# A hybrid RWKV-7 and sparse-attention layer on one core: gates of two token groups projected ahead of the choice of keys, and the choice dealt out differently

## The chip, the core and the metric

The kernel runs on one core of a Trainium2 chip. The metric is device time in microseconds (us) of one execution; the kernel before took 2103.36 us, the median of three runs (2098.55 to 2105.53). The core's engines are PE (matmul, with its weight loads shown as PEld), DVE, ACT, POOL and SP; each works through its own instructions strictly in the order in which the built program holds them. SP issues nearly all DMAs.

## What is computed

One layer on 2048 tokens of width 1024, all in 32-bit floats. `p = rmsnorm(x) @ w_in`, and the columns of `p` go two ways:

```python
p_shift, g_rwkv, q_down, kv_down, k_idx_raw, w_idx, g_attn = jnp.split(p, IN_SPLITS, axis=-1)
y_rwkv = rwkv7_branch(p_shift, g_rwkv, ...)     # r, k, v, decay, a from p_shift; a scan over time; * silu(gate)
y_attn = dsa_branch(q_down, kv_down, k_idx_raw, w_idx, g_attn, ...)
y = jnp.concatenate([y_rwkv, y_attn], axis=-1) @ w_out        # then x + y, and a last rmsnorm
```

The scan runs over 2048 steps with 8 heads of 64. The attention branch first scores all earlier keys of each query with a small index (4 heads of 64), keeps the best 256 of them (`lax.top_k`), and attends to those alone, with 8 heads over a shared latent. Both branches end in a product with `silu` of a gate, 512 columns each (`g_rwkv`, `g_attn`).

## The kernel before

The program has three parts that the scheduler of the framework orders on each engine by priority (the order of the source, unless `later` lowers it) and by its own idea of durations. The result is one fixed order per engine.

**Projections and choice** (`phase_as`). Tokens are worked in four groups of 512. `x_group` (L541) normalises and transposes a group into two tiles `xh`, `xl` (high and low part of the split floats, two buffers each). `proj` (L573) multiplies 128 columns of `w_in` with a group: 24 matmuls of 128x512, eight each on lines 577 to 579, into one of three PSUM tiles `pm`. `load_w` (L524) brings such a weight through one raw buffer and splits it into `wh` (ACT, L535) and `wl` (DVE, L536), three buffers each. `index_proj` and `index_group` (L645, L655) make the index keys, index weights and queries of a group with three projections. A job then uses a finished `pm`: `gate` (L809) takes its SiLU on ACT (L812) and stores it; `shifted`, `keys`, `lora` and `latent` mix neighbouring tokens (L586 on ACT, L588 on DVE), normalise and store.

`visit` (L823) walks over 22 such weights in rounds, each weight for two groups; at its end `x_again` (L567) loads the next two groups. `choose` (L434) makes for each of 14 blocks of 128 queries the scores (L246 and L247 on PE, L249 on ACT, L252 and L254 on DVE; two buffers `xs`) and, at lower priority, `quick` (L271): twelve steps of a search for the threshold, each one pass over the scores with a count, on ACT and POOL for even blocks (L317, L321, L323, L314), on DVE for odd blocks (L320 and the same small lines), and then a tail on DVE (L329 to L346) that fixes ties and stores the block's mask (L347). The blocks come in the order 14, 15, 12, 13, 10, 11, 8, 9, 6, 7, 2, 3, 4, 5. `mix` (L854) takes one share of the choice (one block's scores) after each round of a visit.

```python
for i, g in enumerate(order):            # 2, 3, 0, 1
    t, qr = index_proj(g, ws)
    index_group(g, t, qr)
    if i < 2:
        x_group(order[i + 2])
```

**Scan** (`phase_r`). Sixteen batches of 128 tokens. `prep` (L931, twice a batch) loads `ld` (L937), works on DVE and PE (L950 to L984) and scales on POOL (L987); `systems` sends small triangular systems through DRAM (`du`, then `A`, L1017); `inverse` (L1021) solves them on POOL in 31 steps (L1031, L1033), writes `dx` and reads `TT`; `chain` (L1041) multiplies with `TT` on PE (L1068) and carries the state. Its tiles take the memory of the projections, so it begins when the last projection is finished.

**Attention and output** (`phase_t`, `phase_w`). Units of one head pair and one query block, scores and values by key blocks of 128 (L1261, L1262 scores; L1263 mask and maximum on DVE; L1295 transposes; L1304 value products), then the product with `w_out` (L1381 to L1384). Their priority is lower than the scan's, so they fill its gaps; what is left is done behind it.

Of the kernel before, what the change touches and what calls it, by code (L numbers as in the profile page):

```python
# [475 lines left out]
def phase_as(env):  # L476
# [6 lines left out]
    def tl(shape, dt, tag, bufs=1):  # L483
        return pa.tile(shape, dt, name=nm(tag), tag=tag, bufs=bufs)

    def pst(shape, tag, bufs=1):
        return ps.tile(shape, F32, name=nm(tag), tag=tag, bufs=bufs)

    def t2(dt=F32):
        return tl([128, 512], dt, "t2", 6)  # L490

    def tls(shape, dt, tag, bufs=1):
        return e.ps_.tile(shape, dt, name=nm(tag), tag=tag, bufs=bufs)
# [30 lines left out]
    def load_w(cols, pad=False, raw=None):  # L524

        if raw is None:
            raw = tl([128, KD, 128], F32, "wraw", 1)
        src = e.w_in[0].rearrange("(k p) c -> p k c", p=128)
        if pad:
            G.memset(raw, 0.0)  # L530
        for t0, s0, w in cols:
            dma(raw[:, :, t0:t0 + w], src[:, :, s0:s0 + w])
        wh = tl([128, KD, 128], F32R, "wh", 3)
        wl = tl([128, KD, 128], F32R, "wl", 3)
        S.activation(wh, raw, AF.Copy)  # L535
        V.tensor_tensor(wl, raw, f32(wh), op=OP.subtract)  # L536
        return wh, wl
# [3 lines left out]
    def x_group(g):  # L541
        xh = tl([128, KD, 512], F32R, "xh", 2)
        xl = tl([128, KD, 512], F32R, "xl", 2)
        XH[g], XL[g] = xh, xl
        for tb in range(4 * g, 4 * g + 4):
            xt = tls([128, T], F32, "xs", 2)[:, :D] if tb % 4 >= 2 else tl([128, D], F32, "xt", 2)
            dma(xt, e.x[0, tb * 128:(tb + 1) * 128, :])
            st = tl([128, 4], F32, "xst", 4)
            tcol = slice((tb % 4) * 128, (tb % 4) * 128 + 128)
            S.activation(xl[:, :, tcol], xt.rearrange("p (k c) -> p k c", k=KD), AF.Square, accum_out=st[:, 0:1])  # L550
            V.tensor_scalar(st[:, 1:2], st[:, 0:1], 1.0 / D, 1e-6, op0=OP.mult, op1=OP.add)
            rpow(st[:, 2:3], st[:, 1:2])
            V.scalar_tensor_tensor(xt, xt, st[:, 2:3], gb, op0=OP.mult, op1=OP.mult)
            for hf in range(2):
                pt = pst([128, 4, 128], "tr", 2)
                for k in range(4):
                    kk = hf * 4 + k
                    PE.transpose(pt[:, k], xt[:, kk * 128:(kk + 1) * 128], ident)
                sl = (slice(None), slice(hf * 4, hf * 4 + 4), slice((tb % 4) * 128, (tb % 4) * 128 + 128))
                S.activation(xh[sl], pt, AF.Copy)  # L560
                V.tensor_tensor(xl[sl], pt, f32(xh)[sl], op=OP.subtract)

        if g >= 2:
            dma(e.d_x[g - 2][0], f32(xh))
            dma(e.d_x[g - 2][1], f32(xl))
# [7 lines left out]
    def proj(w, g):  # L573
        wh, wl = w
        pm = pst([128, 512], "pm", 3)
        for k in range(KD):
            PE.matmul(pm, wh[:, k], XH[g][:, k], start=k == 0, stop=False)  # L577
            PE.matmul(pm, wh[:, k], XL[g][:, k], start=False, stop=False)  # L578
            PE.matmul(pm, wl[:, k], XH[g][:, k], start=False, stop=k == KD - 1)  # L579
        return pm  # L580
# [64 lines left out]
    def index_proj(g, ws):  # L645
        t = t2()
        S.activation(t[0:68], proj(ws[0], g)[0:68], AF.Copy)
        qr, sqs = [], []
        for j in range(2):
            pm = proj(ws[1 + j], g)  # L650
            qr.append(t2())
            S.activation(qr[j], pm, AF.Copy)
        return t, qr
# [80 lines left out]
    def latent_weights():  # L734

        raw = tl([128, KD, 128], F32, "wraw", 1).rearrange("p a b -> p (a b)").rearrange("p (a b) -> p a b", a=2)
        dma(raw[:, 0].rearrange("p (h d) -> p h d", h=8), e.w_uk[0].rearrange("h r d -> r h d"))
        dma(raw[:, 1].rearrange("p (h d) -> p h d", h=8), e.w_uv[0].rearrange("h r d -> r h d"))
        for i, n in enumerate(("wh", "wl")):
            ukv[i] = tl([128, KD, 128], F32R, n, 3).rearrange("p a b -> p (a b)").rearrange("p (a b) -> p a b", a=2)  # L740
        split(raw, ukv[0], ukv[1])
# [74 lines left out]
    jobs = dict(kv=([(0, C_KV, 128)], latent), lora=([(0, C_WD, 64), (64, C_WD, 64)], lora))  # L816
# [6 lines left out]
    def visit(gs, rounds, nxt=()):  # L823

        late = []
        for i, names in enumerate(rounds):
            some = [(load_w(jobs[n][0]), jobs[n][1]) for n in names.split()]
            if "kv" in names.split():
                latent_weights()
            for gi, g in enumerate(gs):  # L830
                for w, job in some:
                    pm = proj(w, g)
                    for _ in range(2):
                        if late:
                            late.pop(0)()
                    f = job(pm, g)
                    if f:
                        late += f if isinstance(f, list) else [f]
                if i == len(rounds) - 1:
                    while late:  # L840
                        late.pop(0)()
                    if nxt:
                        x_again(nxt[gi])
            yield

    def index_weights():
        raws = tls([128, 2, KD, 128], F32, "xm", 1)
        ws = [load_w([(0, C_KI, 64), (64, C_WI, 4)], pad=True)]
        if not hasattr(e, "kig"):
            e.__dict__.update(e.vectors())  # L850
            env.update(e.__dict__)
        return ws + [load_w([(0, C_QD + j * 128, 128)], raw=raws[:, j]) for j in range(2)]

    def mix(*gens):  # L854

        while next(gens[0], gens) is not gens:
            for x in gens[1:]:
                next(x, None)

    order = (2, 3, 0, 1)  # L860
    x_group(2)
    ws = index_weights()
    query_weights()
    x_group(3)
    for i, g in enumerate(order):
        t, qr = index_proj(g, ws)
        index_group(g, t, qr)
        if i < 2:
            x_group(order[i + 2])
    lora_weights()  # L870
    stored = dma(e.d_ki, f32(KI))
    with tc.issue_after(stored.ins):
# [3 lines left out]
    shares = choose((7, 6, 5, 4, 3, 1, 2))  # L876
    for _ in range(2):
        next(shares)
    mix(visit((0, 1), ["r0 gr0 k0", "lora v0 ga0", "kv r1", "gr1 k1", "v1 ga1", "r2 gr2", "k2 v2", "ga2 r3", "gr3 k3",
                       "v3 ga3"], (2, 3)), shares)  # L880
    mix(visit((2, 3), ["r0 gr0 k0", "lora v0 ga0", "kv r1", "gr1 k1", "v1 ga1", "r2 gr2", "k2 v2", "ga2 r3 gr3",
                       "k3 v3 ga3"]), shares)
    for _ in shares:
        pass

# [534 lines left out]
```

## Time and profile before

| | us |
|---|---|
| median of three runs | 2103.36 |
| the profiled execution | 2104.7 |
| its span in the profile | 2102.9 |
| PE busy / weight loads busy | 1803.3 (86%) / 1421.8 (68%) |
| DVE busy | 1296.7 (62%) |
| ACT busy | 1019.8 (48%) |
| POOL busy | 795.3 (38%) |

The span is the time from the first to the last instruction of the program; 1.8 us of the execution lie around it. Busy times are unions of an engine's instructions; matmuls overlap in their pipeline, so PE's is not a measure of its work. A row of a view of time windows gives for each engine its busy us and (after x) its number of instructions, then the granted share of PE's clock (1.00 is 2.4 GHz, 0.50 is 1.2 GHz; a stretch between shows both), the DMA engines' busy share and GB/s.

### The profile page before, as it was taken

Reading aid. Unit: us, or ns where it says so; the run is one execution under the profiler, and the core shown is the slowest. Engines: PE = TensorE matmul, PEld = TensorE weight load, DVE = VectorE, ACT = ScalarE, POOL = GpSimd, SP = SyncE. Lnnn points to the kernel's source line nnn. Section 1 sums busy time; section 2 is a strip of 40 time slices with the busy share of each in tenths; the row PEclk is TensorE's granted clock in tenths of the full one; section 3 lists DMA queues with packets and bytes.
Section 4 is the critical chain, followed back from the end, with each engine's and each line's share of the span. In section 5 each row is a group of like instructions: output and inputs, shape, how many; then the busy total and the mean of one; then the engine's idle time right before and its main releaser. Section 6 shows DMA issues by size and latency. Waiting matters only on the chain.

```text
span 2102.9 us, 36153 instructions
## 1 busy us (share of the span) xinstructions
PE 1803.3 (86%) x12906; PEld 1421.8 (68%) x12906; DVE 1296.7 (62%) x3050; ACT 1019.8 (48%) x1966; POOL 795.3 (38%) x1925
## 2 busy tenths in 40 slices
PE   5788998879796988986788988886988889899998
PEld 4666877658575867765566766665766667587776
DVE  5532538979779698986656557564756654644432
ACT  4422494453444744441355555454655567643431
POOL 1110124353544354562445645654546650100000
PEclk9778999989798999998799998798988899999999
DMA  7526334332262434234844355343454324744223
GB/s 248 199 94 200 108 101 135 101 115 85 75 239 63 135 107 136 91 95 125 204 102 105 95 136 147 105 119 98 115 143 131 93 78 108 233 128 128 66 93 112
DMA packets 309038, 262.50 MB, mean 125 GB/s; under 512 B 82544, under 2 KB 258288, under 8 KB 307696
## 3 DMA queue, kind: packets, MB, share of 16 engines
q1 hardware_dynamic: 304464, 248.03, 40.1%
q0 software_dynamic: 4384, 12.06, 1.8%
q8 instruction: 104, 1.70, 0.4%
q14 instruction: 86, 0.70, 0.1%
HBM read 166.37 MB, written 97.85 MB: 126 GB/s over the span
## 4 chain that ended last, share of the span: by engine, by line
PE 23%; POOL 14%; DMA 12%; issue 5%; DVE 4%; SPq 1%; ACT 1%; POOLq 0%; DVEq 0%; ACTq 0%
DMA A<-du 6%; POOL Xr L1033 6%; POOL Xtmp L1031 5%; PE om L1304 3%; PE po L1381 3%; PE po L1382 3%; PE po L1384 3%; PE tr L1295 3%; DMA dx<-Xr 2%; PE s L1261 2%; PE s L1262 1%; DMA TT<-dx 1%; DMA ld<-d_rw 1%; POOL yo L1129 1%; POOL gst L1112 1%
## 5 line engine op out<-in xcount | busy, mean ns | idle before, releaser
L577 PE MATMUL pm<-xh,wh 128*128 128x512 f32 x800 | 330.4, 414 | 20.3 <-DVE t L588 11.8
L578 PE MATMUL pm<-xl,wh 128*128 128x512 f32 x800 | 327.0, 409 | 0.0
L579 PE MATMUL pm<-xh,wl 128*128 128x512 f32 x800 | 326.1, 408 | 0.0
L1263 DVE CUSTOM_DVE_ANT_0 sc<-s,mk 128x512 f32<-128x512 f32 (+3 forms) x320 | 187.9, 607 | 102.8 <-PE s L1262 76.0
L1297 ACT ACTIVATE pt<-tr 128x512 f32<-128x512 f32 (+1 forms) x288 | 157.9, 569 | 160.8 <-PE tr L1295 115.9
L1031 POOL TENSOR_TENSOR Xtmp<-Xr,A 128x60 f32<-128x60 f32 (+24 forms) x496 | 146.9, 296 | 225.8 <-DMA A<-du 181.8
L577 PEld LDWEIGHTS pm<-xh,wh 128*128 128x128 f32 x800 | 158.1, 198 | 61.7 <-DVE t L588 13.7
L1270 ACT ACTIVATE sc<-sc,mx 128x128 f32<-128x128 f32 (+15 forms) x128 | 153.0, 1198 | 63.0 <-DVE mx L1269 62.7
L1295 PE MATMUL tr<-ident,sc 128*128 128x128 f32 x1088 | 180.1, 292 | 3.0 <-ACT pt L1297 2.6
L579 PEld LDWEIGHTS pm<-xh,wl 128*128 128x128 f32 x800 | 157.3, 197 | 36.4
L578 PEld LDWEIGHTS pm<-xl,wh 128*128 128x128 f32 x800 | 158.0, 197 | 35.4
L1304 PE MATMUL om<-pt,vt 128*64 128x128 f32 x2176 | 174.0, 295 | 6.2 <-DVE ga L1287 6.2
L1261 PE MATMUL s<-kt,q 128*128 128x512 f32 (+2 forms) x320 | 144.2, 454 | 35.8 <-DVE mx L1263 32.2
L1033 POOL TENSOR_TENSOR Xr<-Xr,Xtmp 128x60 f32<-128x60 f32 (+24 forms) x496 | 151.3, 305 | 37.4
L1304 PEld LDWEIGHTS om<-pt,vt 128*64 128x64 f32 x2176 | 134.2, 146 | 37.6 <-issue 19.6
L1295 PEld LDWEIGHTS tr<-ident,sc 128*128 128x128 f32 x1088 | 133.5, 149 | 33.9 <-issue 11.4
L317 ACT ACTIVATE mk<-x,st 128x1920 bf16<-128x1920 f16 (+5 forms) x72 | 98.0, 1361 | 103.6 <-POOL st L314 103.6
L249 ACT ACTIVATE rl<-lg,wi 128x512 f32<-128x512 f32 (+3 forms) x152 | 94.0, 631 | 99.6 <-PE lg L247 53.1
L1262 PE MATMUL s<-kt,q 128*128 128x512 f32 (+2 forms) x320 | 123.3, 389 | 8.1 <-DMA q<-d_q 8.0
L320 DVE TENSOR_SCALAR_CACHE_REDUCE mk<-x,st 128x2048 bf16<-128x2048 f16 (+5 forms) x72 | 120.6, 1675 | 1.4
L254 DVE SCALAR_TENSOR_TENSOR xs<-rl,wi,xs 128x512 f32<-128x512 f32 (+3 forms) x108 | 73.5, 681 | 60.9 <-ACT rl L249 60.1
L1387 POOL TENSOR_TENSOR st<-st 128x1 f32<-128x1 f32 x16 | 3.1, 195 | 277.1 <-ACT po L1386 277.1
(329 smaller groups left out, 3937.7 us busy)
## 6 DMA issues: line engine op xcount, KB each, us to landing
wraw<-in_w_in_dram SPq DMA_DIRECT2D x42, 512.0 KB
d_rw<-t SPq DMA_DIRECT2D x80, 256.0 KB
ld<-d_rw SPq DMA_DIRECT2D x32, 640.0 KB
q<-d_q SPq DMA_DIRECT2D x128, 128.0 KB
d_q<-t SPq DMA_DIRECT2D x32, 256.0 KB
d_kt<-t SPq DMA_DIRECT2D x32, 256.0 KB
kt<-d_kt SPq DMA_DIRECT2D x32, 256.0 KB
A<-du SPq DMA_DIRECT2D x16, 512.0 KB
```

The costliest lines, as they stand in the source:

```text
L577: PE.matmul(pm, wh[:, k], XH[g][:, k], start=k == 0, stop=False)
L578: PE.matmul(pm, wh[:, k], XL[g][:, k], start=False, stop=False)
L579: PE.matmul(pm, wl[:, k], XH[g][:, k], start=False, stop=k == KD - 1)
L1031: G.tensor_tensor(tmp[:, :m, :w], Xr[:, :m, s:s + 1].to_broadcast([128, m, w]), A[:, s:s + 1, s + 1:].to_broadcast([128, m, w]), op=OP.mult)
L1033: m_ = G.tensor_tensor(Xr[:, :m, s + 1:], Xr[:, :m, s + 1:], tmp[:, :m, :w], op=OP.add)
L1261: PE.matmul(pS[:, :wp], qh[:, h, qs], k[:, h, :wp], start=True, stop=False)
L1262: PE.matmul(pS[:, :wp], ql[:, h, qs], k[:, h, :wp], start=False, stop=True)
L1263: V.tensor_tensor_reduce(out=rows[h][:, c0:c0 + w], in0=pS[:, :w], in1=mk[:, c0:c0 + w], scale=1.0, scalar=LOW, op0=OP.add, op1=OP.max, ac ...
L1270: marks[p, b] = S.activation(rows[h][:, :n], rows[h][:, :n], AF.Exp, bias=mx[:, h, 4:5], accum_out=sums[:, h:h + 1]).ins
L1295: PE.transpose(pt[:, i, h], rows[h][:, (kb + i) * 128:(kb + i) * 128 + 128], ident)
L1297: S.activation(w[:, :m], pt[:, :m], AF.Copy)
L1304: PE.matmul(po[HALF[h]], v[:, (kb + i) % 4, HALF[h]], w[:, i, h], start=kb + i == 0, stop=kb + i == b)
```

## The change

The eight gate weights (`gr0` to `gr3`, `ga0` to `ga3`) of groups 2 and 3 are taken out of the second visit and projected in a function of their own, `gates`, between the index groups of 2 and 3 and the loading of groups 0 and 1. The index weights are loaded a second time behind them, since the gates use their buffers. The second visit has 14 weights in 7 rounds instead of 22 in 9. `mix` skips a share after two rounds of the first visit (numbers 3 and 6) and after three of the second (2, 4 and 6).

```diff
-    def mix(*gens):
-
-        while next(gens[0], gens) is not gens:
-            for x in gens[1:]:
-                next(x, None)
+    def mix(main, other, skip):
+
+        for i, _ in enumerate(main):
+            if i not in skip:
+                next(other, None)
+
+    def gates(gs, rounds):
+
+        for names in rounds:
+            some = [(load_w(jobs[n][0]), jobs[n][1]) for n in names.split()]
+            for g in gs:
+                for w, job in some:
+                    job(proj(w, g), g)
...
-    for i, g in enumerate(order):
+    for g in order[:2]:
         t, qr = index_proj(g, ws)
         index_group(g, t, qr)
-        if i < 2:
-            x_group(order[i + 2])
+    gates(order[:2], ["gr0 ga0 gr1", "ga1 gr2", "ga2 gr3 ga3"])
+    ws = index_weights()
+    for g in order[2:]:
+        x_group(g)
+    for g in order[2:]:
+        t, qr = index_proj(g, ws)
+        index_group(g, t, qr)
...
     mix(visit((0, 1), ["r0 gr0 k0", "lora v0 ga0", "kv r1", "gr1 k1", "v1 ga1", "r2 gr2", "k2 v2", "ga2 r3", "gr3 k3",
-                       "v3 ga3"], (2, 3)), shares)
-    mix(visit((2, 3), ["r0 gr0 k0", "lora v0 ga0", "kv r1", "gr1 k1", "v1 ga1", "r2 gr2", "k2 v2", "ga2 r3 gr3",
-                       "k3 v3 ga3"]), shares)
+                       "v3 ga3"], (2, 3)), shares, (3, 6))
+    mix(visit((2, 3), ["r0 k0", "lora v0 r1", "kv r2", "r3 v1", "v2 v3", "k1 k2", "k3"]), shares, (2, 4, 6))
```

The order on the engines changes with it; lines behind L860 have numbers 12 higher in the changed file. On ACT, behind the queries of group 3 (L623, from `pm`): before, the copies of the transposed tokens of group 1 (L560) and the next index projection (L647) follow.

```order
L623 ACTIVATE t_142_848<-pm_841 128x512
L560 ACTIVATE xh_867<-tr_918 128x4x128
L623 ACTIVATE t_145_861<-pm_854 128x512
L560 ACTIVATE xh_867<-tr_925 128x4x128
L560 ACTIVATE xh_867<-tr_939 128x4x128
L647 ACTIVATE t_165_953<-pm_954 68x512
```

In the changed program, at the same place, the gates' SiLUs (L812) and weight splits (L535) stand, and the tokens of group 0 behind them:

```order
L623 ACTIVATE t_127_775<-pm_768 128x512
L812 ACT_TABLE_LOAD
L812 ACTIVATE t_139_824<-pm_799 128x512
L812 ACTIVATE t_141_852<-pm_827 128x512
L812 ACTIVATE t_143_880<-pm_855 128x512
L535 ACTIVATE wh_969<-wraw_967 128x1024
...
L812 ACTIVATE t_182_1246<-pm_1221 128x512
L521 ACTIVATE w2s_134<-wraw_1878 128x1024
L535 ACTIVATE wh_1292<-xm_1277 128x1024
L812 ACTIVATE t_184_1274<-pm_1249 128x512
L560 ACTIVATE xh_1296<-tr_1305 128x4x128
```

All sixteen gates of the two groups moved there; on PE their projections stand in one run behind the last query projection of group 3.

On SP's queue, where the scan begins (`ld`, `vt`), before: the stores of the last projections (`d_rw`, `d_v`, `d_ga`), the scan's first loads, and attention's first loads (`kt`).

```order
L813 DMA d_ga<-t_1340_7737 128x512
L798 DMA d_rw<-t_1336_7702 128x512
L806 DMA d_v<-t_1338_7708 128x512
L937 DMA ld_7779<-d_rw 128x10x128
L943 DMA vt_7780<-d_v 128x2x128
...
L1124 DMA gr_8762<-d_gr 128x2x128
L1221 DMA kt_13715<-d_kt_68 64x2x512
```

In the changed program the masks of blocks 7, 2 and 3 (L347, 1024, 384 and 512 keys) are stored between the last projection's stores and the scan's first load; those of blocks 4 and 5 and the first write of `dx` come ahead of attention's first load:

```order
L347 DMA d_mask_78<-mk_5656 128x1024
L798 DMA d_rw<-t_1348_7756 128x512
L347 DMA d_mask_73<-xt_5953 128x384
L347 DMA d_mask_74<-xt_6360 128x512
L949 DMA ld_7798<-d_rw 128x10x128
...
L347 DMA d_mask_75<-mk_6984 128x640
...
L1046 DMA dx_7887<-Xr_7888 4x256x32
L347 DMA d_mask_76<-mk_7548 128x768
L1050 DMA TT_7958<-dx_7887 32x8x32 x4
...
L1233 DMA kt_13734<-d_kt_68 64x2x512
```

The end of the choice moved behind the end of the projections, and the scan's first load behind the mask of block 3.

## Rows read from the trace of the kernel before

**Rows 1.** Time windows by stage: window, its length, then busy us by engine.

```profile
core 0: us, PE busy (x) PEld busy (x) DVE busy (x) ACT busy (x) POOL busy (x), PEclk, DMA share, GB/s
0.00:201.00 201.00, 150.59 (x664) 120.49 (x665) 91.45 (x210) 72.69 (x132) 23.63 (x36) 0.85 0.53 178
201.00:601.00 400.00, 353.44 (x1507) 280.27 (x1506) 282.92 (x407) 208.73 (x288) 152.42 (x266) 0.92 0.36 116
601.00:979.00 378.00, 331.81 (x1457) 265.13 (x1455) 321.86 (x651) 173.70 (x289) 187.43 (x381) 0.94 0.34 111
979.00:1068.00 89.00, 53.99 (x314) 40.15 (x313) 50.33 (x175) 30.26 (x81) 27.06 (x89) 0.73 0.80 193
1068.00:1740.00 672.00, 571.04 (x6579) 445.07 (x6580) 393.71 (x1209) 371.77 (x848) 377.54 (x1093) 0.88 0.43 112
1740.00:2100.00 360.00, 342.44 (x2392) 270.70 (x2390) 156.41 (x399) 162.69 (x330) 27.26 (x62) 0.98 0.41 126
```

**Rows 2.** Time windows of line 577 alone (PE, then weight loads).

```profile
201.00:601.00 400.00, 146.57 (x353) 70.12 (x353) 0.92 0.36 116
601.00:979.00 378.00, 144.86 (x352) 69.19 (x351) 0.94 0.34 111
```

**Rows 3.** Timeline of PE inside a projection: start, us, instruction.

```profile
937.61 0.39 PE L577 MATMUL pm<-xh,wh 128*128 128x512 f32 x1
...
939.01 0.39 PE L577 MATMUL pm<-xh,wh 128*128 128x512 f32 x1
```

**Rows 4.** Timelines of DVE, SP, POOL and PE at the end of the phase.

```profile
959.93 0.96 DVE L331 MAX8 st<-xm 128x8 f32<-128x768 f32 x1
...
966.09 0.56 DVE L346 TENSOR_TENSOR mk<-mk,eq 128x768 bf16<-128x768 bf16 x1
...
979.76 0.74 DVE L588 SCALAR_TENSOR_TENSOR t<-pm,om_r,m 128x512 f32<-128x512 f32 x1
...
981.01 0.58 SPq L937 DMA_DIRECT2D ld<-d_rw  x1
...
1024.96 0.24 POOL L1031 TENSOR_TENSOR Xtmp<-Xr,A 128x31 f32<-128x31 f32 x1 [18.57 <-DMA A<-du]
...
1068.11 0.41 PE L1068 MATMUL ch<-R,TT 32*32 32x64 f32 x2 [8.40 <-DMA TT<-dx]
```

**Rows 5.** Waits of 1050 to 1740 (total, times, longest), and line 1031 on its own.

```profile
POOL Xtmp L1031 <- DMA A<-du: 163.2, 13, 17.2
...
L1031 POOL TENSOR_TENSOR Xtmp<-Xr,A x496: 209/292/745, 1025.0 to 1730.1; 128x60 f32<-128x60 f32 x16, 128x28 f32<-128x28 f32 x12, 128x66 f32<-128x66 f32 x11, 128x48 f32<-128x48 f32 x10
```

**Rows 6.** Time windows in the holes of the early stage.

```profile
95.00:110.00 15.00, 8.38 (x39) 7.00 (x39) 11.35 (x28) 7.87 (x17) 5.15 (x6) 0.61 0.00 0
116.00:126.00 10.00, 4.66 (x25) 4.13 (x23) 2.24 (x4) 1.18 (x3) 0.68 (x1) 0.66 0.68 211
...
180.30:192.30 12.00, 6.49 (x32) 5.58 (x31) 6.76 (x19) 4.09 (x8) 2.02 (x2) 0.64 0.35 90
```

**Rows 7.** Groups by line and form on DVE, 201 to 979: busy, mean ns.

```profile
L536 DVE TENSOR_TENSOR wl<-wraw,wh 128x1024 fp32r<-128x1024 f32 x41 | 50.1, 1222 | 24.0 <-ACT wh L535 24.0
```

**Rows 8.** Groups by line on ACT, 201 to 979.

```profile
L535 ACT ACTIVATE wh<-wraw 128x1024 fp32r<-128x1024 f32 x41 | 43.3, 1055 | 44.2 <-DMA wraw<-in_w_in_dram 26.8 <-PE pm L578 15.2 <-PE pm L579 2.0
...
L812 ACT ACTIVATE t<-pm 128x512 f32<-128x512 f32 x32 | 18.9, 591 | 26.2 <-PE pm L579 16.3 <-DMA d_kt<-t 9.7 <-PE tr L776 0.2
```

**Rows 9.** Groups by line and form on DVE, 890 to 979: a search step of block 5.

```profile
L320 DVE TENSOR_SCALAR_CACHE_REDUCE mk<-x,st 128x768 bf16<-128x768 f16 x12 | 12.1, 1008 | 0.3
...
L314 DVE TENSOR_SCALAR st<-st 128x1 f32<-128x1 f32 x15 | 4.1, 271 | 0.9 <-POOL st L312 0.5
...
L321 DVE TENSOR_SCALAR st<-st 128x1 f32<-128x1 f32 x16 | 3.4, 210 | 0.3
```

**Rows 10.** Timeline of PE in the last stage: value products and transposes of attention.

```profile
1898.40 1.97 PE L1304 MATMUL om<-pt,vt 128*64 128x128 f32 x32
...
1903.17 1.09 PE L1295 MATMUL tr<-ident,sc 128*128 128x128 f32 x8
```

## Prediction

> **What bounds the kernel now.** I read the profile from coarse to fine: the stages of the span, then who holds up whom at the two seams that the change touches.
>
> The page gives one busy share per engine over the whole span, a mean over stages with different limits; the busy time by stage [rows 1] separates them. From 0 to 201 us, while the four groups are prepared, DVE works 91 us of 201 and PE has holes. From 201 to 601 (visit of groups 0 and 1) and from 601 to 979 (visit of groups 2 and 3) the projections and the choice of keys share the engines: DVE is busy 283 of 400 us, then 322 of 378. From 979 the scan starts alone; from 1068 to 1740 its chain runs with attention filled in; after 1740 PE does attention and the output product at 342 of 360 us.
>
> That the visits are these stretches is seen by counting: a projection has 8 matmuls of line 577, and the two visits hold 353 and 352 of them [rows 2], which is 44 projections each; the early stage has the 12 of the index. A projection at full clock costs 24 matmuls that start 0.233 us apart (937.61 to 939.01 for six) [rows 3], so 5.6 us. The 44 of the second visit are thus 246 us of PE in 378; the matmuls' busy time of 332 us is larger because they overlap. DVE's 322 us do not overlap. **In the second visit DVE is nearer to its limit than PE.**
>
> By the raw busy row PE (332) would lead DVE (322), and taking gates out would give PE's share back: that is the second case below, 2110 us. The Trainium skill (Perfetto Trace Analysis, "Identifying the Most-Contended Engine") says that matmul busy time is no measure of PE's headroom, and to take the weight loads' busy share there and plain occupancy for VectorE. Here that gives 265 of 378 (70%) against 85%, so by that rule VectorE leads and the forecast, 2150 us, is the one to take. The same page ("Optimization Strategy") advises interleaving regimes with different limits, which speaks against a stretch of gates by themselves.
>
> At the end of the phase the last DVE operation of the choice ends at 966.7, the last shift of a projection on DVE starts at 979.76, SP issues the scan's first load at 981.01, the first triangular inverse starts on POOL at 1024.96 and the first product with it on PE at 1068.11 [rows 4]. The scan's stage is then paced by a loop through POOL and DMA: POOL waits 163 us there for A [rows 5].
>
> **The change, part by part.** The profiled execution took 2104.7 us (span 2102.9); the median of the three runs is 2103.4, so sums on the profile are 1.3 us high.
>
> 1. *Sixteen gates go in front of the choice.* The choice of the first blocks needs the index keys of all four groups, so all of it, and both visits, start later by what the gates take. In the built order they stand in one block after the index group of group 3, not in the holes of the early stage (95 to 110, 116 to 126, 180.3 to 192.3, where PE is busy 20 of 37 us [rows 6]). Sixteen at 5.6 us are 90 us. The two token loads of groups 0 and 1 stood in the holes of groups 2 and 3; now they stand behind the gates, whose last three projections cover their squares. What the hole of group 3 loses in width (it runs on to 126 [rows 6]) comes back behind the gates. I take plus 90, ends 78 and 102: the visits start at 291 instead of 201.
>
> 2. *Weights.* Eight gate weights are split earlier (8 x 1.22 us of DVE [rows 7], 8 x 1.06 of ACT [rows 8]) and three index weights are loaded once more, 512 KB each, through SP's queue during the gates. A split frees the weight buffer after at most 2.3 us and the gates use a weight for 11.2 us, so PE covers them: 0. Without that cover the three would cost 3 x 2.3 = 7 us. The gates' sixteen SiLUs (0.59 us [rows 8]) and stores go with them; they run beside PE: 0.
>
> 3. *First visit.* Its rounds are unchanged, and on DVE the built order has the choice at the same places between the same projections: block 13 ends before the last key projection in both, although two shares are skipped, since only two score buffers exist. So 400 us again, until 691.
>
> 4. *Second visit.* Twenty-eight projections are left. DVE's work behind the start of the visits is 283 + 322 = 605 us [rows 1]; 10 us of weight splits leave it. In the built order SP stores the mask of block 3 ahead of the scan's first load, and blocks 4 and 5 end on DVE after that; ten of twelve search steps of block 5 (1.01 us each, and three small operations of 0.21 to 0.27 [rows 9]: 18 us) and two block tails (that of block 5 ran from its pass for the largest values at 959.93 to 966.65 [rows 4], 6.7 us, and one pass more stands ahead of it: 15 us for two) are left behind the load, 33 us in all. So 605 - 10 - 33 - 283 = 279 us of DVE must pass between 691 and the load. At the second visit's 85% that takes 328 us, without any idle 279. PE has 16 x 5.6 = 90 us less to do there, so some of DVE's waits for PE go, but those inside the choice (score to ReLU to sum, POOL to ACT) stay. I take 90%: 310 us, and the load at about 1003: **plus 22** against 981. Ends with those of part 1: minus 15 and plus 50.
>
> 5. *Head of the scan.* Before, 87 us lie between the first load and the first product, at a DMA share of 0.80 [rows 1] because attention's loads run in front on the same queue. Now those loads come behind the first inverse, but 33 us of DVE work and the last POOL steps of block 4 come in front of it. Both unknown; the idle in that stretch is 39 of 89 us on DVE, so most of the 33 fits: 0, ends minus 12 and plus 15.
>
> 6. *Attention starts later.* It now begins behind the first product instead of well ahead of it. On PE the built order has 742 of the 1088 value products of attention ahead of the scan's last matmul, 816 before: 74 more are left, which is 37 pairs of a query and a key block. One pair is 8 products of 64 columns in the trace's halves (1.97 us for 32 records: 0.25 us), two transposes (1.09 us for 8: 0.27) and 512 columns of scores (0.23) [rows 10]: 0.75 us, 28 in all, at the end where PE has 18 of 360 us idle. I take **plus 24**, ends 10 and 28. From the second pair of scan batches to the last, the built order has 694 products before and 688 now, so the loop between keeps its pace.
>
> Sum: 2104.7 + 22 + 0 + 24 = 2151, about **2150 us** as a median. Its own range, part by part, is 2122 to 2182.
>
> **The other ways it could go.**
>
> *PE was the limit of the second visit.* Then DVE runs without idle once the gates are gone: load at 291 + 400 + 283 = 974, minus 7; the head gains 10 without attention's loads; attention's remainder still costs 24: about 2110 us. For it: PE waits little in the second visit, 332 of 378 busy. Against: 246 us of projections in 378, and DVE at 85%.
>
> *Faster: the scan's stage is paced by PE.* Besides the case just told (load 974, head minus 10), the 37 pairs taken out of the stage would shorten it by the 28 us that they cost later, so the two cancel: 2104.7 - 7 - 10 = about 2088. It decides from an inverse cadence under 44 us; now the 16 x 31 steps run from 1025.0 to 1730.1 [rows 5], some 45 us a batch. For it: PE busy 571 of 672 [rows 1]. Against: the 163 us for which POOL waits for A [rows 5].
>
> *Slower still: the head is stretched.* POOL's and DVE's in-order queues put block 4's and block 5's serial steps between the scan's preparations, each waiting for the other; plus 15 in the head, the load at the far end, plus 50: about 2190. For it: from 1068 to 1740, where two kinds of work share every queue as they would here, no engine but PE is busy for 60% (DVE 394 of 672 us) [rows 1]. Against: PE and ACT are nearly free in the head.
>
> That the change does not do what it says is half a rival: the gates fill no hole, and the choice is hardly spread. Both are in the forecast.
>
> **How the numbers follow.** Forecast (2122 to 2182) 0.58; PE the limit 0.15; faster 0.10; slower still 0.17. Of the second case, which lies at plus 0.3% with some 10 us either way, I count 0.07 as no change (within 0.3%, or 6 us, about what a measurement can tell) and 0.08 as slower. Slower: 0.58 + 0.17 + 0.08 = 0.83; same 0.07; faster 0.10. For eight in ten the range reaches down to the second case and up to the near side of the fourth: 2108 to 2186.
>
> **What would show it.** In the new profile: a stretch of 16 gates with PE full and DVE nearly empty, some 90 us; the first scores of the choice near 300; the second visit shorter than 378 us but by less than 90; the scan's first load near 1003, behind the store of block 3's mask; the first attention score after the first inverse; cadence of the inverses unchanged; more attention behind the scan's end. The prediction is wrong if the scan's first load comes before 980, or if the visits start before 275.

## The result and the profile after

The changed kernel takes 2169.07 us (median; 2166.88 to 2171.27), the kernel before, run beside it, 2100.95 (2097.73 to 2105.53): a ratio of 1.0323, with a 95% interval of 1.0307 to 1.0339, so it is slower by 68 us. The forecast was 2150, its range 2108 to 2186. The profiled execution has a span of 2167.2 us and took 2169.0.

The busy time of the profile after by stage, with the columns of [rows 1]. The first row and the third make up the early stage of before with the gates in it, and the row of 114 to 204 is the gates alone:

```profile
0.00:294.00 294.00, 242.88 (x1048) 193.47 (x1049) 105.80 (x221) 94.13 (x160) 23.68 (x37) 0.89 0.48 155
...
114.00:204.00 90.00, 90.00 (x391) 73.00 (x390) 16.82 (x18) 23.20 (x34) 4.01 (x5) 1.00 0.25 79
204.00:294.00 90.00, 75.28 (x319) 58.68 (x318) 38.75 (x75) 30.74 (x56) 7.67 (x10) 0.79 0.41 129
...
294.00:696.00 402.00, 354.13 (x1508) 280.59 (x1507) 285.13 (x410) 208.40 (x288) 154.88 (x267) 0.92 0.36 117
696.00:948.00 252.00, 228.22 (x1010) 183.22 (x1009) 218.68 (x387) 125.55 (x203) 124.62 (x254) 0.95 0.37 123
948.00:1014.00 66.00, 17.18 (x64) 12.50 (x62) 62.09 (x179) 22.16 (x48) 44.36 (x96) 0.53 0.09 34
1014.00:1097.00 83.00, 29.16 (x148) 20.74 (x148) 58.76 (x162) 13.48 (x33) 42.93 (x121) 0.52 0.36 96
1097.00:1741.00 644.00, 542.77 (x6177) 422.17 (x6175) 393.72 (x1198) 359.19 (x835) 356.17 (x1027) 0.88 0.49 123
1741.00:2167.00 426.00, 399.76 (x2959) 314.02 (x2959) 183.69 (x501) 200.86 (x401) 48.86 (x128) 0.97 0.39 119
```

Read it from the top. For 90 us PE does gates without a pause while DVE is busy 17: that stretch is new. The first visit is as long as before (402 against 400). The projections of the second visit end at 948, 252 us after its start instead of 378. But then comes a stretch that the kernel before did not have: from 948 to 1014 DVE is busy 62 of 66 us, PE 17, at a granted clock of 0.53. The projections' matmuls are done and the choice is not.

The seam, by the timelines of DVE (ends of blocks 7, 2, 3, 4 and 5), SP, POOL and PE (the second PE row is attention's first score):

```profile
983.80 0.68 DVE L346 TENSOR_TENSOR mk<-mk,eq 128x1024 bf16<-128x1024 bf16 x1
995.43 0.35 DVE L346 TENSOR_TENSOR xt<-xt,eq 128x384 bf16<-128x384 bf16 x1
1012.65 0.41 DVE L346 TENSOR_TENSOR xt<-xt,eq 128x512 bf16<-128x512 bf16 x1
1049.99 0.47 DVE L346 TENSOR_TENSOR mk<-mk,eq 128x640 bf16<-128x640 bf16 x1
1083.87 1.45 DVE L346 TENSOR_TENSOR mk<-mk,eq 128x768 bf16<-128x768 bf16 x1
...
1013.10 0.32 SPq L347 DMA_DIRECT2D d_mask<-xt  x1
1013.58 0.59 SPq L949 DMA_DIRECT2D ld<-d_rw  x1
1085.34 7.73 SPq L347 DMA_DIRECT2D d_mask<-mk  x1
1094.99 1.78 SPq L1050 DMA_DIRECT2D TT<-dx  x4
...
1097.47 1.25 SPq L1233 DMA_DIRECT2D kt<-d_kt  x2
...
1056.20 0.24 POOL L1043 TENSOR_TENSOR Xtmp<-Xr,A 128x31 f32<-128x31 f32 x1 [11.86 <-DMA A<-du]
...
1096.79 0.42 PE L1080 MATMUL ch<-R,TT 32*32 32x64 f32 x2 [8.92 <-DMA TT<-dx]
1106.86 0.77 PE L1273 MATMUL s<-kt,q 128*128 128x256 f32 x2 [0.81 <-DMA ga<-d_ga]
```

Against [rows 4]: the choice's last operation starts at 1084 instead of 966, the scan's first load is issued at 1013.6 instead of 981.0, right behind the store of block 3's mask, and attention's first load at 1097. On SP that one stands behind the store of block 5's mask, whose issue took 7.73 us, and behind the scan's own loads of `TT`, so here both the choice's end and the first inverse lie just ahead of it; e7 separates them. The span divides into four: the load 32.6 us later; from the load to the first product 83.2 us instead of 87.1; from there to the scan's last product 727.4 instead of 724.5; behind it 343.0 instead of 310.3. Sum: 32.6 - 3.9 + 2.9 + 32.7 = 64.3, the difference of the spans.

What the last term is made of shows in the PE groups behind the scan's last product, first after (from 1824), then before (from 1792): transposes and value products of attention.

```profile
L1307 PE MATMUL tr<-ident,sc 128*128 128x128 f32 x338 | 54.3, 283 | 4.5 <-ACT pt L1309 4.0 <-ACT sc L1282 0.5
L1316 PE MATMUL om<-pt,vt 128*64 128x128 f32 x692 | 49.1, 283 | 1.7 <-DVE ga L1299 1.7
```

```profile
L1295 PE MATMUL tr<-ident,sc 128*128 128x128 f32 x266 | 40.2, 277 | 1.0 <-ACT pt L1297 0.9
L1304 PE MATMUL om<-pt,vt 128*64 128x128 f32 x544 | 37.9, 284 | 1.5 <-DVE ga L1287 1.5
```

692 value products instead of 544 are left, 148 more, which is 4 for each of the 37 pairs that the prediction counted.

### The profile page after: what moved, and what is told of

Same layout as the page of the kernel before. It is cut to its first block, busy times and chain, and to the rows that moved or that the text cites. A ratio compares the mean times of both kernels' runs of the same rounds, so it can differ in the third digit from the quotient of the medians.

```text
span 2167.2 us, 36188 instructions
## 1 busy us (share of the span) xinstructions
PE 1814.1 (84%) x12906; PEld 1426.7 (66%) x12906; DVE 1307.9 (60%) x3053; ACT 1023.8 (47%) x1964; POOL 795.5 (37%) x1926
## 4 chain that ended last, share of the span: by engine, by line
PE 34%; POOL 21%; DMA 14%; DVE 14%; issue 9%; ACT 5%; SPq 2%; POOLq 0%; ACTq 0%; DVEq 0%
POOL Xr L1045 6%; POOL Xtmp L1043 6%; DMA A<-du 6%; PE pm L577 4%; PE pm L578 4%; PE pm L579 4%; PE po L1393 3%; DVE mk L320 3%; PE po L1394 3%; PE po L1396 3%; PE om L1316 2%; PE tr L1307 2%; PE s L1273 2%; DMA dx<-Xr 2%; ACT mk L317 1%
## 5 line engine op out<-in xcount | busy, mean ns | idle before, releaser
L1316 PE MATMUL om<-pt,vt 128*64 128x128 f32 x2176 | 167.1, 291 | 2.3 <-DVE ga L1299 2.3
L1316 PEld LDWEIGHTS om<-pt,vt 128*64 128x64 f32 x2176 | 129.3, 144 | 32.9 <-issue 20.1
L536 DVE TENSOR_TENSOR wl<-wraw,wh 128x1024 fp32r<-128x1024 f32 x46 | 56.2, 1222 | 86.8 <-ACT wh L535 86.8
```

The costliest lines, as they stand in the source:

```text
L1316: PE.matmul(po[HALF[h]], v[:, (kb + i) % 4, HALF[h]], w[:, i, h], start=kb + i == 0, stop=kb + i == b)
```

## The experiments

Three theories stood against each other. **The choice** (its work on DVE, with POOL and ACT) ends when it ends, whatever PE has to do, and the scan and attention wait for it. **PE's projections** set the phase. **The order** that the change brings with it (dealing, mask stores on SP, keys last) is the cost. In the table "first pass" is the start of the choice's first L292 on DVE, "choice ends" its last L346; all times are of one profiled execution of each, in us; the ratio is of the medians, to the kernel before on the same chip. "Left" counts value products of attention behind the scan's last product.

| kernel | ratio, 95% interval | first pass | choice ends | scan's first load | attention's first score | scan's last product | behind it | left |
|---|---|---|---|---|---|---|---|---|
| before | 1 | 254.9 | 966 | 981 | 997 | 1793 | 310 | 544 |
| after | 1.0323 [1.0307, 1.0339] | 347.8 | 1084 | 1014 | 1107 | 1824 | 343 | 692 |
| e1, no dealing | 1.0319 [1.0302, 1.0337] | 345.8 | 1081 | 1011 | 1103 | 1814 | 343 | 692 |
| e2, dealing alone | 0.9994 [0.9985, 1.0004] | 255.3 | 965 | 979 | 996 | 1786 | 310 | 544 |
| e3, before, thin gates | 0.9832 [0.9815, 0.9849] | 250.0 | 1006 | 925 | 1017 | 1723 | 340 | 676 |
| e4, after, thin gates | 1.0196 [1.0179, 1.0213] | 303.7 | 1040 | 970 | 1061 | 1768 | 362 | 776 |
| e5, before, short search | 0.9824 [0.9799, 0.9849] | 251.4 | 849 | 941 | 958 | 1747 | 309 | 544 |
| e6, after, short search | 0.9973 [0.9957, 0.9990] | 346.4 | 963 | 975 | 991 | 1781 | 309 | 544 |
| e7, no spare tiles | 1.0390 [1.0357, 1.0423] | 349.6 | 1147 | 992 | 1166 | 1781 | 392 | 908 |
| e8, masks on POOL | 1.0362 [1.0336, 1.0388] | 348.6 | 1084 | 988 | 1102 | 1813 | 361 | 776 |
| e9, keys early | 1.0343 [1.0314, 1.0372] | 347.9 | 1095 | 1010 | 1104 | 1812 | 358 | 724 |
| e10, before, keys late | 1.0122 [1.0090, 1.0155] | 253.7 | 956 | 1000 | 1016 | 1810 | 311 | 544 |
| e11, eight gates | 1.0168 [1.0139, 1.0197] | 299.7 | 1038 | 974 | 1059 | 1786 | 339 | 692 |
| e12, block 3 on ACT | 1.0018 [1.0000, 1.0036] | 254.3 | 962 | 986 | 1002 | 1787 | 314 | 568 |

**Gates or dealing (e1, e2).** e1 is the changed kernel with the share taken every round; e2 the kernel before with the changed dealing.

```diff
-    mix(visit((0, 1), [...], (2, 3)), shares, (3, 6))
-    mix(visit((2, 3), [...]), shares, (2, 4, 6))
+    mix(visit((0, 1), [...], (2, 3)), shares, ())
+    mix(visit((2, 3), [...]), shares, ())
```

> The gates stand where the change puts them, but the choice is dealt one share a round as before. Theory (the 16 gates ahead of the choice are the whole loss, the dealing none): 2159 to 2179 us, scan's first load within 8 us of the 1013 of the changed kernel. Rival (the dealing carries a good part of the loss, or gives some of it back): under 2150 or over 2190 us.

> The gates stand where they stood before, only the choice is dealt with the skipped rounds. Theory (dealing costs nothing, because two score buffers hold the choice at the same places anyhow): 2093 to 2109 us. Rival (dealing carries a part of the loss): 2115 us or more.

Measured: 2163.18 us, load at 1011, and 2095.22 us. Both as the theory had it: the dealing is nothing, and the loss comes with the gates.

**Thin gates (e3, e4).** The sixteen gates keep one of eight groups of three matmuls, so neither kernel computes them whole. The lines are e4's; e3 makes the same cut inside `visit`, for the gates of groups 2 and 3 alone.

```diff
-    def proj(w, g):
+    def proj(w, g, kd=KD):
...
-        for k in range(KD):
+        for k in range(kd):
...
-                    job(proj(w, g), g)
+                    job(proj(w, g, 1), g)
```

> Kernel before, but each of the 16 gates of groups 2 and 3 keeps only 3 of its 24 matmuls (the rest of that product is left out). That takes 16 x 21 x 0.233 = 78 us of PE out of the second visit; DVE's work is the same. Theory (the choice's chain on DVE, POOL and ACT limits that visit): the scan's first load comes at most 30 us earlier than 981, total 2070 to 2098 us. Rival (PE's projections limit it): the load near 910, total 2020 to 2045 us.

> Changed kernel, with the same 21 of 24 matmuls left out of the same 16 gates. Theory (ahead of the choice each microsecond of a gate is on the path): the visits start near 216 instead of 294, everything behind it moves up by the same 78 us, total 2085 to 2100 us, so the two thin kernels lie within 25 us of each other where the full ones lie 68 apart. Rival (the loss is not the gates' PE time, but the changed order behind it: the mask stores ahead of the scan's load, the weights loaded twice): total over 2115 us.

Measured: 2062.50 and 2137.19 us. In e3 neither side was met. The load came 56 us earlier, so 78 us of PE taken out of the second visit come back for more than two thirds: PE does count there. But the choice ended later, not earlier (1006 against 966), so attention started 92 us behind the scan's load instead of 16, and what is left behind the scan grew by 29 us. The load went, the choice stayed, as SP's timeline and line 346 on DVE (how often, least, median and greatest ns, first and last start) show:

```profile
925.22 0.59 SPq L937 DMA_DIRECT2D ld<-d_rw  x1
...
L346 DVE TENSOR_TENSOR mk<-mk,eq x12: 480/852/1216, 353.7 to 1006.5; 128x1920 bf16<-128x1920 bf16 x1, 128x2048 bf16<-128x2048 bf16 x1, 128x1664 bf16<-128x1664 bf16 x1, 128x1792 bf16<-128x1792 bf16 x1
```

e4 lies where its rival had put it (over 2115), and the thin kernels are 75 us apart, not under 25: moving the gates costs about as much thin as whole. Only 44 of the 78 us came off ahead of the choice. The window of its gates:

```profile
114.00:154.00 40.00, 18.80 (x58) 11.67 (x56) 9.79 (x13) 19.18 (x30) 4.02 (x6) 0.70 0.57 164
```

PE is busy 19 of 40 us, and of the idle time ahead of its projections 18 end with a weight's split on ACT: without the matmuls the stretch lasts 40 us instead of 90 - 78 = 12. Part 2 of the prediction named that cover and priced its absence from the splits alone (7 us); the weights' loads in front of the splits cost more (on ACT, 11 us of waits for `wraw` in this window). In the thin kernel the weights pace the stretch; in the whole one they are covered, since 16 x 5.6 = 90 us of matmuls account for the 92.9 us by which the first pass is later. So what e4 pays for in front is not what the changed kernel pays for. The 44 us then reach the scan's load in full (970 against 1014), and attention, with 84 more products left than in the changed kernel, gives 19 of them back behind the scan.

**Short search (e5, e6).** Six search steps instead of twelve.

```diff
-STEPS = 12
+STEPS = 6
...
-        V.tensor_scalar(flag, rows[0:1, 0:1], 0.5, None, op0=OP.is_gt)
+        V.tensor_scalar(flag, rows[0:1, 0:1], 1.0e9, None, op0=OP.is_gt)
```

> Kernel before, with 6 search steps a block instead of 12 (the thresholds are coarser, so the masks are not those of the reference; the second pass never runs). On DVE that takes out 6 counts and 12 small operations for each of the 7 blocks it searches, about 83 us over both visits, and as many steps on ACT and POOL. Theory, with what the thin gates showed (78 us of PE out of the second visit brought the scan's load 55 us forward, so the two in-order queues wait for each other and both count): load 20 to 60 us before 981, total 2045 to 2080 us. Rival (PE alone paces the visits): load less than 10 us earlier, total over 2085 us.

> The same 6 steps in the changed kernel. Theory (from 948 to 1014 only the choice is left, DVE 62 of 66 us busy and PE 17, and attention cannot start before the choice's last block ends at 1084, so a shorter choice counts in full there): load 45 us or more before 1013, total 2080 to 2120 us, under 55 us above the short kernel before, where the full ones lie 68 apart. Rival (the choice is no more of a limit here than before): 60 us or more above the short kernel before.

Measured: 2059.46 and 2092.66 us, 33 apart, where the full kernels lie 68 apart. e5 fits the theory (load 40 us earlier). The window of its second visit up to the load:

```profile
595.00:939.00 344.00, 319.01 (x1424) 254.86 (x1423) 225.04 (x430) 140.44 (x224) 148.72 (x286) 0.97 0.36 118
```

DVE is down to 225 of 344 us, PE up to 319: without half of the search PE is the fuller engine. In e6 the total fits, the load does not: 38 us earlier, where 45 or more was expected; there the choice's last tail no longer holds it, but the row norm of the last key (its store at 974.60, the load at 975.08). The gain beyond that is at the other seam. The choice ends at 963, ahead of the load, as the view of line 346 shows:

```profile
L346 DVE TENSOR_TENSOR mk<-mk,eq x12: 492/845/1211, 416.2 to 963.4; 128x1920 bf16<-128x1920 bf16 x1, 128x2048 bf16<-128x2048 bf16 x1, 128x1664 bf16<-128x1664 bf16 x1, 128x1792 bf16<-128x1792 bf16 x1
```

Among PE's groups behind the scan's last product stands:

```profile
L1316 PE MATMUL om<-pt,vt 128*64 128x128 f32 x544 | 38.8, 288 | 1.6 <-DVE ga L1299 1.6
```

Attention starts as early as before (27 us ahead of the first inverse in both) and leaves the same 544 products. The whole plus of 33 us behind the scan is gone, with the gates still in front. So the late end of the choice makes that plus, not the gates' place as such.

**The memory that the scan waits for (e7).** Blocks 2 and 3 in ordinary buffers.

```diff
-        if n <= 512:
+        if spare and n <= 512:
...
-    setup_s, choose = picker(e, tls, KI, wi_a, wi_s, True, spare)
+    setup_s, choose = picker(e, tls, KI, wi_a, wi_s, True)
```

> Changed kernel, but blocks 2 and 3 of the choice use the ordinary score buffers instead of two tiles in the projections' memory, so the scan's memory is free without them. Theory (the scan's start waits for the choice in that memory, and attention's start for the choice's end): the first load moves forward to 965 to 1000, the choice ends at 1080 or later, so the scan's end gains up to 30 us, and what is left of attention behind it grows; total 2135 to 2170 us. Rival (DVE's order holds the scan's head anyway): first load earlier, but first inverse within 8 us of 1056, total within 8 us of the changed kernel.

Measured: 2177.78 us, outside both. The mechanism came as the theory had it: load at 992, first inverse at 1030 instead of 1056, the scan's last product 43 us earlier. But the choice, in two buffers and beside the scan, ended only at 1147, and attention's first loads stand right behind its last mask, by SP's timeline:

```profile
1157.18 0.40 SPq L347 DMA_DIRECT2D d_mask<-mk  x1
1157.63 1.45 SPq L1050 DMA_DIRECT2D TT<-dx  x3
1159.12 1.27 SPq L1233 DMA_DIRECT2D kt<-d_kt  x2
```

There the first inverse had started at 1030 and the first product with it at 1079, so it is the choice's end that attention waits for. And among PE's groups behind the scan's last product:

```profile
L1316 PE MATMUL om<-pt,vt 128*64 128x128 f32 x908 | 64.1, 283 | 0.0
```

908 products are left, and 392 us behind the scan: plus 49, which is more than the 43 that were gained.

**The queue that the load stands in (e8).**

```diff
-        dma(e.d_mask[b], mk[:, :n])
+        (dma if n > 1024 else G.dma_start)(e.d_mask[b], mk[:, :n])
```

> Changed kernel, but the mask stores of blocks 2 to 7 are issued on POOL's queue instead of SP's, so that the scan's loads do not stand behind them on SP. Theory (the load at 1013 follows the end of block 3 at 1012.7 because that block lies in the projections' memory, not because of SP's queue): load within 6 us of 1013, total within 8 us of the changed kernel. Rival (SP's order holds the load): load near 990, right behind the last store of a projection, total 2140 to 2155 us.

Measured: 2174.29 us; the load at 988 as the rival said, the total within the theory's 8 us (5 apart; by the ratios, 1.0362 and 1.0323, about 8). SP's order did hold the load, but the load was not what the scan waited for, by the timelines of SP and DVE:

```profile
987.88 0.58 SPq L949 DMA_DIRECT2D ld<-d_rw  x1
...
1018.40 1.01 DVE L320 TENSOR_SCALAR_CACHE_REDUCE mk<-x,st 128x768 bf16<-128x768 f16 x1
1019.34 0.08 DVE L320 DVE_READ_ACCUMULATOR mk<-x,st 128x1 f32 x1
1019.34 0.69 DVE L962 TENSOR_TENSOR_SCAN L<-restart,ld 128x256 f32<-128x256 f32 x1
```

The load was issued at 988, and DVE came to the scan's first operation at 1019.34, behind block 3 and a count of block 5 in its queue; in the changed kernel that operation started at 1019.3 too.

e8 also bounds what the choice's end explains. It ends at 1084 as in the changed kernel, and attention starts 5 us earlier, yet 776 products are left instead of 692. In e4 776 are left with the choice's end at 1040, and in e11, below, 692 with its end at 1038. Which products stand behind the scan's last one is fixed in the built order, and these runs do not show what in the order makes the difference between 692 and 776.

**Keys first or last (e9, e10).** The change put the keys at the end of the second visit. e9 gives them three projections as cover, e10 puts them last in the kernel before.

```diff
-    mix(visit((2, 3), ["r0 k0", "lora v0 r1", "kv r2", "r3 v1", "v2 v3", "k1 k2", "k3"]), shares, (2, 4, 6))
+    mix(visit((2, 3), ["r0 k0", "lora v0 r1", "kv r2", "r3 v1", "k1 k2", "k3 v2", "v3"]), shares, (2, 4, 6))
```

```diff
-    mix(visit((2, 3), ["r0 gr0 k0", "lora v0 ga0", "kv r1", "gr1 k1", "v1 ga1", "r2 gr2", "k2 v2", "ga2 r3 gr3",
-                       "k3 v3 ga3"]), shares)
+    mix(visit((2, 3), ["r0 gr0 k0", "lora v0 ga0", "kv r1", "gr1 r2", "v1 ga1", "gr2 r3", "v2 ga2", "gr3 v3 ga3",
+                       "k1 k2 k3"]), shares)
```

> Changed kernel, with the last rounds of the second visit in another order: keys 1 to 3 no longer come last but have three value projections behind them, so their row norms (the last store of a key at 987.9, 40 us after the last projection) run beside PE. Theory (the choice's work on DVE sets the end of the phase, 62 of 66 us busy there): the scan's load within 8 us of 1013, total within 10 us of the changed kernel. Rival (the keys' chains at the end push the choice back, an order that the change brought with it): load 985 to 1000, total 2125 to 2150 us.

> Kernel before, with all its projections, but keys 1 to 3 last and gates ahead of them, the mirror of the run before. Theory (as there): up to 15 us more at the end of the second visit, since there the choice ends first (966) and the last keys' norms have only DVE's rest to wait for; total 2095 to 2112 us. Rival (the place of the keys carries the loss): load 25 us or more after 981, total over 2120 us.

Measured: 2167.53 us, with the load at 1010: as the theory had it, the keys' place is not the loss. And 2122.53 us: over the theory's 2112 and, in the total, where the rival had it (over 2120), with the load 19 us later (1000; the rival had 25 or more) although the choice ended 10 us earlier (956). There the keys' norms are the last thing (the last key's store at 999.44), 27 us behind the last projection's last matmul (972.5). So the order of the keys costs where PE's work ends last, and is hidden where the choice does.

**Half the gates in front (e11).**

```diff
-    gates(order[:2], ["gr0 ga0 gr1", "ga1 gr2", "ga2 gr3 ga3"])
+    gates(order[:2], ["gr0 ga0 gr1", "ga1"])
...
-    mix(visit((2, 3), ["r0 k0", "lora v0 r1", "kv r2", "r3 v1", "v2 v3", "k1 k2", "k3"]), shares, (2, 4, 6))
+    mix(visit((2, 3), ["r0 k0", "lora v0 r1", "kv r2", "gr2 v1", "r3 k1", "ga2 v2", "gr3 k2", "v3 ga3", "k3"]), shares, (2, 4, 6))
```

> Changed kernel, with 8 of the 16 gates (numbers 0 and 1 of each kind, of both groups) ahead of the choice and the other 8 back in the second visit. Theory (each gate in front costs its 5.6 us and gives about two thirds back behind): visits start near 249, load near 997, half of the loss, total 2120 to 2142 us. Rival 1 (up to some number the gates are free, because DVE only becomes the limit when most of them are gone): under 2110 us. Rival 2 (what costs is the stretch itself, with its weights loaded twice): over 2150 us.

Measured: 2127.41 us, half of the loss, as expected, but not by the expected road. The choice's first passes and last operations, each line on its own:

```profile
L292 DVE TENSOR_REDUCE vm<-xs x12: 701/2469/3852, 299.7 to 946.6; 128x256 f32<-128x1792 f32 x2, 128x256 f32<-128x1536 f32 x2, 128x256 f32<-128x1280 f32 x2, 128x256 f32<-128x1024 f32 x2
L346 DVE TENSOR_TENSOR mk<-mk,eq x12: 483/850/1222, 403.0 to 1038.2; 128x1920 bf16<-128x1920 bf16 x1, 128x2048 bf16<-128x2048 bf16 x1, 128x1664 bf16<-128x1664 bf16 x1, 128x1792 bf16<-128x1792 bf16 x1
```

The scan's first load, by SP's timeline:

```profile
973.92 0.58 SPq L949 DMA_DIRECT2D ld<-d_rw  x1
```

The same line 292 before and after:

```profile
L292 DVE TENSOR_REDUCE vm<-xs x12: 676/2444/3892, 254.9 to 904.9; 128x256 f32<-128x1792 f32 x2, 128x256 f32<-128x1536 f32 x2, 128x256 f32<-128x1280 f32 x2, 128x256 f32<-128x1024 f32 x2
...
L292 DVE TENSOR_REDUCE vm<-xs x12: 684/2472/3892, 347.8 to 992.6; 128x256 f32<-128x1792 f32 x2, 128x256 f32<-128x1536 f32 x2, 128x256 f32<-128x1280 f32 x2, 128x256 f32<-128x1024 f32 x2
```

The load was expected at 997 and came at 974, 7 us *before* that of the kernel before. The 45 us of the eight gates in front came back behind in full, and 7 more: from the first pass to the load it takes 726 us before, 674 with eight gates out, 675 in e3 and 666 in the changed kernel. The other eight give back 8 of their 45 us. (The order of the rounds differs too: in e11 a key stands last, and the load follows its store at 973.44.) The choice, from its first pass to its end, takes 711 us before, 738 here, 736 in the changed kernel, 756 in e3: taking gates out never makes it shorter, and in these three, where it ends beside the scan, it takes 25 to 45 us longer. Half of the gates cost nothing at the load and 29 us behind the scan (692 products are left, as many as with all sixteen).

**An attempt to be faster (e12).**

```diff
-        return b % 2 == 0
+        return b % 2 == 0 or b == 3
```

> Kernel before, gates in their old place, but the search of block 3 (12 counts of 0.74 us and 24 small operations of 0.21 to 0.27 us, 15 us of DVE) runs on ACT and POOL. An attempt at a faster kernel. Theory (DVE and PE both pace the second visit, and the shorter search brought the load 40 us forward for some 83 us of DVE in both visits): load 3 to 10 us earlier, total 2084 to 2096 us. Rival (PE paces it, or the longer chain through ACT and POOL takes it back): 2096 to 2106 us.

Measured: 2099.62 us, a ratio of 1.0018, as the rival had it. The choice ends 4 us earlier, the load comes 5 us later: 15 us less of DVE do not bring the load forward. Whether PE holds it there or the longer chain through ACT and POOL took the gain back, this run does not separate. No version among these that computes the whole beats the kernel before.

## Why the prediction was right, and where its steps were off

The direction and the mechanism held, and the time lies in the forecast's own range. The 19 us by which 2150 fell short are two terms of the sum that were mis-sized. The forecast was chosen over its rivals by an argument on PE and DVE that was wrong for the kernel before, so that it came out right was in part luck. Its own range, 2122 to 2182, does not follow from the ends that its parts give: read as shifts against the profile before, they add up to 2088 and 2198.

- *Part 1, gates in front: plus 90.* Held: 114 to 204 with PE full and DVE at 17 of 90 us; the first pass of the choice 92.9 us later. That the dealing adds nothing is shown by e1 and e2, that the keys' new place adds nothing by e9.
- *Part 2, weights: 0.* Held as long as the gates' matmuls cover them; in e4, without that cover, the stretch is 28 us longer than its matmuls' share.
- *Part 3, first visit: 400 us again.* 402.
- *Part 4, the load: plus 22; measured plus 32.6.* The work was right: 281 us of DVE (219 and 62 in the rows of 696 to 1014) against the 279 that the step counted. The pace was not: 281 of 318 us is 88%, not 90%, which is 8 us; the visit also began 5 us later than 691, and the prediction had rounded 691 + 310 up to 1003.
- *The argument for part 4, "DVE is nearer to its limit than PE" in the second visit.* It holds for the changed kernel from 948 on; for the kernel before it does not. PE's 332 us are not 246 us of projections made longer by overlap: the visit holds 1457 matmuls [rows 1], 401 besides the 1056 of its 44 projections. And the weight loads' share cannot be set against DVE's as it stands: where PE has no pause at all (114 to 204 after, 391 matmuls in 90 us) they are busy 73 of 90 us, 81%. On that scale 265 of 378 us are some 86% of what PE can do, an estimate from these two rows, against 85% for DVE. The runs agree that both count: eight gates out bring the load 52 us nearer to the first pass (e11), half of the search out brings it 40 us forward (e5). By the rule of the Trainium skill that the prediction leaned on (Perfetto Trace Analysis, "Identifying the Most-Contended Engine"), weight loads at 70% against DVE at 85% make DVE the bound of that stage; e11 does not agree with it for this load, and the measurement decides. The second visit has two ends, the load and the choice's last block, and one busy share cannot tell which engine holds which.
- *Part 5, head of the scan: 0.* Minus 3.9, inside its bounds; e8 shows DVE's queue, not the load, to be what holds the scan's first operation there.
- *Part 6, attention later: plus 24; measured plus 32.7.* The count was exact (37 pairs, 148 records); the price was low: 32.7 us over 37 pairs is 0.88 us each instead of 0.75. e7 gives 82 us for 364 records, 0.90 a pair, and e8 51 us for 232, 0.88. The step saw in the order that attention is late; that it follows from the choice's end is shown by e6 (choice early: the plus is gone) and e7 (choice later still: the plus more than doubles). That the count is exact is no measure of the wait: it is read off the built order, which also gives the 776 of e4 and e8.
- *The rivals.* "PE was the limit of the second visit" was true of the kernel before in part (e11, e5) and still did not give 2110, since the choice takes over as the limit (its 974 also counts 283 us of DVE where part 4 has 279). The scan paced by PE: the inverses follow 45.6 us apart, 45.4 before, so no. "The head is stretched" in its form did not come (83 us), but in the head the choice's last two blocks are stretched instead, and attention pays for it.

## What to carry to other kernels

Work that is moved to where it stands alone costs its full length at once; what it gives back where it stood is bounded by the next limit there, and that limit can be passed halfway, so try half of the move before judging all of it. When a stage hands on two things (here the projections' results to the scan, and the masks to attention), find for each the engine that holds it and the consumer that waits: here eight gates brought the first forward at no loss, while the second got later whenever gates were taken out or thinned. And price a late start by what it leaves for the end, where nothing covers it: about 0.9 us a pair in three kernels here, 0.8 in e11 and 1.1 in e9.

## What the runs showed of the hardware

Some operations of POOL and DVE that ran at the same time took longer than alone. In the head of the changed kernel one step of the inverse on POOL takes 1.64 us beside a DVE scan and ends with it, where the median of that line is 0.297; and DVE's last sum of block 5, 0.56 us in the kernel before [rows 4], took 1.45 us in the row of 1083.87 above, beside two multiplications on POOL:

```profile
1078.50 1.64 POOL L1045 TENSOR_TENSOR Xr<-Xr,Xtmp 128x35 f32<-128x35 f32 x1
1083.86 2.35 POOL L999 TENSOR_TENSOR BK<-BK,eC 128x512 f32<-128x512 f32 x2
...
1078.33 1.76 DVE L343 TENSOR_TENSOR_SCAN xm<-eq 128x768 f32<-128x768 bf16 x1
```

The scan runs from 1078.33 to 1080.09, the step from 1078.50 to 1080.14. The Trainium skill (SBUF — State Buffer, "Who interferes with whom") says that the port pair which DVE shares with GpSimd (POOL) is an exclusive lock, and that a DVE instruction with two inputs in SBUF contends there with a GpSimd instruction that reads SBUF. These rows agree: the scan is given `eq` as both of its inputs, the sum `mk` and `eq`. That this is why the choice's last blocks take longer beside the scan was not tried by itself.

Where PE had little to do its granted clock was lower, and the short work that then lay on the path ran at it: 0.53, near the lower of the two levels (1.2 of 2.4 GHz), from 948 to 1014 and 0.52 from 1014 to 1097, with PE busy 17 of 66 and 29 of 83 us, against 0.73 in the head of the kernel before [rows 1], where attention kept it busy 54 of 89. What the lower clock cost was not tried by itself.
